# Where a diffusion trunk computes its adaLN modulation: as fills of the RWKV stage on TensorE, or on VectorE during the first projection

## The chip, the cores and the metric

The kernel runs on one core of one Trainium2 chip. The metric is device microseconds of one execution. A core has a matmul engine (TensorE, PE in the views), three elementwise engines (VectorE or DVE, ScalarE or ACT, GpSimd or POOL) and a queue engine (SyncE, SP) that here issues every transfer. Weights are loaded into the matmul engine by separate instructions (PEld in the views), which overlap with running matmuls.

## The reference, cut to what matters

One inference step over 128 context tokens and 1,024 latent tokens, width 1,024, two layers. Each layer norms its input, modulates it, projects it for four parallel mixers, mixes, projects back and adds the result through a gate. All three parts of the modulation are linear in a conditioning vector:

```python
sc_ctx = silu(c_ctx)             # context tokens
sc     = silu(c)                 # latent tokens
for l in range(2):
    mod = sc @ w_mod[l] + b_mod[l]          # (1024) @ (1024, 3072); once with sc_ctx, once with sc
    shift, scale, gate = split(mod, 3)      # 1024 each
    h = rmsnorm(x, norm_g[l]) * (1 + scale) + shift
    u = h @ w_in[l]                         # mLSTM, RG-LRU, retention, RWKV-7 inputs
    y = concat(mlstm(u), rglru(u), retention(u), rwkv(u)) @ w_out[l]
    x = x + gate * y
y = rmsnorm(x, final_g)
```

## The kernel before, in words

Activations lie with features on the 128 partitions and the 1,152 tokens along the rows. A layer has two long stages.

**First projection stage.** `in_proj` works through the list `JOBS` (one job for each block of 128 output features, or two blocks): 44 of its 56 jobs, since the RWKV inputs of head pairs 1 to 3 are left for later. A job loads its weights, splits them in two parts (ACT and POOL), and for each slice of 384 tokens accumulates 24 matmuls into a bank of PSUM with the tag `main`, of which there are two. DVE and ACT take turns to copy the bank to `st`, which is stored to memory. The mixers mLSTM, RG-LRU and retention (functions `ml_pair`, `lr_pair`, `rt_pair`, four head pairs each, one after the other) read these stores back and run on all engines at a higher priority, so the matmuls of `in_proj` fill what they leave free on TensorE.

**RWKV stage.** `rw_all` runs a long chain of small dependent steps. Here the order of the instructions on TensorE is written out by hand: a generator `work()` yields one matmul after the other of other work (the *fills*, line 1296), and `rw_all` pulls some of them at each step of its chain, so many that they last until its end (`nfill` is their number). The fills are the late RWKV projections (`late_proj`), the output projection (`out_proj`) and, in layer 0 alone, eight of the twelve blocks of the modulation. `tail` ends the layer.

**The modulation** has six blocks of 512 columns for each layer. Blocks 0 to 3 of layer 0 (shift and scale) are needed first and computed at the very start (`modulation0`). The other eight (`MODS`: the gate of layer 0, all of layer 1) are computed by `modulation`, in groups ahead of the late projections of pair 1, 2 and 3. `mod_rows` does a block: eight loads of 128 x 512 weights into the six buffers `ow`, eight fills with the two conditioning vectors (`silu_c`, 128 x 2) as TensorE's weights and the 512 columns streaming, which gives a row of 2 x 512; an ACT copy; four transposes; and a DVE addition of the bias into `mod`.

A float32 matmul is two instructions on TensorE here, so that a block's eight fills stand in the trace as 16 passes.

Outside the hand-made order a planner, which plays the program through on a timeline, orders each engine's instructions by priority: without a `high_priority` they come in the order of the code, with an offset of `HP1` or `HP2` ahead of that (`level(1)` is `HP1`, which is also what the mixers have; the copies of the projection have `HP2`).

Of the kernel before, what the change touches and what calls it, by code (L numbers as in the profile page):

```python
# [9 lines left out]
F32 = mybir.dt.float32  # L10
# [6 lines left out]
MUL, ADD, SUB, MAX, MIN = ALU.mult, ALU.add, ALU.subtract, ALU.max, ALU.min  # L17
# [13 lines left out]
class B:  # L31
# [1059 lines left out]
    def mod_rows(self, l, j, pool, w, n, pr, pc, mm, between=lambda k: None):  # L1091


        row_ps = pr()
        for k in range(0, 8, n):
            wt = w()
            self.dma(wt, self.i["w_mod"][l, j][:, k:k + n])
            between(k // n)
            for z in range(n):
                mm(row_ps[0:2], self.sc[:, k + z], wt[:, z], start=(k + z == 0), stop=(k + z == 7))  # L1100
                if k + z < 7:
                    yield
        row = pool.tile([2, 512], F32, tag="mrow", name="mrow", bufs=1)
        self.a.copy(row, row_ps[0:2])
        col_ps = pc()[:, 0:8].rearrange("p (i c) -> p i c", c=2)
        for i in range(4):
            self.tr(col_ps[:, i], row[:, 128 * i:128 * i + 128])
        self.tt(self.v, self.mod[l][:, 4 * j:4 * j + 4], col_ps,
                self.par["bmod"][:, 24 * l + 4 * j:24 * l + 4 * j + 4, None].broadcast_to([128, 4, 2]), ADD)
        yield  # L1110

    def modulation(self, l, j, pool):

        w = lambda: pool.tile([128, 1, 512], F32, tag="ow", name="wmod")
        yield from self.mod_rows(l, j, pool, w, 1, self.pmain, self.pmain, self.fill)

    def modulation0(self, pool, ps, between):

        bank = lambda n: lambda: ps.tile([128, 512], F32, tag=n, name=n)
        w = lambda: pool.tile([128, 2, 512], F32, tag="w0", name="w0", bufs=8)  # L1120
        for j in range(4):
            for _ in self.mod_rows(0, j, pool, w, 2, bank("row"), bank("col"), self.mm, lambda k: between(2 * j + k // 2) if k % 2 else None):
                pass

    def scales(self, l, pool):

# [120 lines left out]
        self.a.copy(hi, raw)  # L1247
        self.tt(self.g, lo, raw, hi.bitcast(F32), SUB)

    def in_proj(self, l, wp, sp, hh, hl):  # L1250
        n = 0
        rh = wp.tile([128, 3, KT, 128], F32R, name="wring_h")
        rl = wp.tile([128, 3, KT, 128], F32R, name="wring_l")
        pos = 0
        for t_, (kind, name, p, tiles) in enumerate(JOBS):
            if name[:3] == "rw_" and p in LATE:
                continue
            nt = len(tiles)
            if pos + nt > 3:
                pos = 0  # L1260
            with self.tc.high_priority(offset=HP2):
                for z, t in enumerate(tiles):
                    raw = wp.tile([128, KT, 128], F32, tag="raw", name="raw", bufs=2)
                    self.dma(raw, self.i["w_in"][l, t])
                    self.split_w(raw, rh[:, pos + z], rl[:, pos + z])
            hi, lo = rh[:, pos:pos + nt], rl[:, pos:pos + nt]
            pos += nt
            if kind == "C":
                dst = self.U[l, name, p] = self.dr0.tile([128, T], F32, name="u_%s_%d_%d" % (name, p, l))
                units = [(dst[:, o:o + CH3], slice(o, o + CH3), CH3) for o in range(0, T, CH3)]  # L1270
            else:
                dst = self.U[l, name, p] = self.dr0.tile([9, 128, 256], F32, name="ut_%s_%d_%d" % (name, p, l))
                units = [(dst[i], slice(128 * i, 128 * i + 128), 256) for i in range(9)]
            for d, s, w in units:
                ps = self.pmain()
                j = 0
                for k in range(KT):
                    for a, b in ((hi, hh), (hi, hl), (lo, hh)):
                        if kind == "C":
                            x, y = a[:, 0, k], b[:, k, s]  # L1280
                        else:
                            x, y = b[:, k, s], a[:, :, k]
                        self.mm(ps[:, :w], x, y, start=(j == 0), stop=(j == 3 * KT - 1))
                        j += 1
                with self.tc.high_priority(offset=HP2):
                    q = sp.tile([128, CH3], F32, tag="st", name="st", bufs=3)
                    if n % 2:
                        self.a.copy(q[:, :w], ps[:, :w])  # L1288
                    else:
                        self.v.tensor_copy(q[:, :w], ps[:, :w])  # L1290
                    n += 1
                    self.dma(d, q[:, :w])
# [66 lines left out]
    def build(self):  # L1359
# [10 lines left out]
        for l in range(2):  # L1370
# [6 lines left out]
            with self.ph as ph:  # L1377
                P = lambda n, b=1, **kw: ph.enter_context(tc.tile_pool(name=n + "_%d" % l, bufs=b, **kw, **tw))
                wp, sp = P("w"), P("st")
                self.in_proj(l, wp, sp, *self.h)  # L1380
                with tc.high_priority(offset=HP1), ExitStack() as st:
                    Q = lambda n, b=1, **kw: st.enter_context(tc.tile_pool(name=n + "_%d" % l, bufs=b, **kw, **tw))
                    self.mlrow = self.dr.tile([2, 40, T], F32, tag="mlrow", name="mlrow")
                    self.mldec = self.dr.tile([40, 9], F32, tag="mldec", name="mldec")
                    self.xps = Q("xps", 1, space=PSUM)
                    self.mp = Q("mp", **R)
                    self.ml_layer(l)
                    self.mq = Q("mq", **R)
                    for p in range(4):
                        self.ml_pair(l, p)  # L1390
                    with ExitStack() as st2:
                        Q = lambda n, b=1, **kw: st2.enter_context(tc.tile_pool(name=n + "_%d" % l, bufs=b, **kw))
                        self.lp = Q("lp", **R)
                        self.lr_layer(l, self.load_cols(self.lp, l, ("cw", "cb", "lam", "gb", "h0"), "lr_"))
                        self.lq = Q("lq", **R)
                        for p in range(4):
                            self.lr_pair(l, p)
                    with ExitStack() as st2:
                        Q = lambda n, b=1, **kw: st2.enter_context(tc.tile_pool(name=n + "_%d" % l, bufs=b, **kw))
                        self.tp = Q("tp", **R)  # L1400
                        self.rt_layer(l)
                        self.tq = Q("tq", **R)
                        for p in range(4):
                            self.rt_pair(l, p)
            fin = ExitStack()
            self.rf = fin.enter_context(tc.tile_pool(name="rw_fin_%d" % l, bufs=1, **R, **tw))
            with ExitStack() as ph:
                P = lambda n, b=1, **kw: ph.enter_context(tc.tile_pool(name=n + "_%d" % l, bufs=b, **kw, **tw))
                self.mainps = P("mo", 2, space=PSUM)
                wp, yp, sp = P("wo", OWB), P("yo", YOB), P("so", SO)  # L1410
                with tc.high_priority(offset=HP1):
                    self.rl, self.rp = P("rw_lora", **R), P("rw_pair", **R)
                    self.rt, self.rd = P("rw_tmp"), (P("rw_even"), P("rw_odd", **R))
                    self.rps = P("rw_ps", space=PSUM)
                    self.rw_layer(l, self.load_cols(self.rl, l, ("mu", "w0", "a0", "kk", "ka", "rk"), "rw_"))

                def work():
                    for p in LATE:
                        for z, j in MODS[p] if l == 0 else ():
                            yield from self.modulation(z, j, wp)  # L1420
                        yield from self.late_proj(l, p, wp, yp, sp)
                    yield from self.out_proj(l, ((0, 4), (1, 4), (2, 4)), wp, yp, sp)
                    while self.finished < 4:
                        yield
                    yield from self.out_proj(l, ((3, 3),), wp, yp, sp)
                    self.done.add("all")

                self.fills, self.done, self.credit, self.pulled, self.finished = work(), set(), 0.0, 0, 0
                self.nfill = 648 + (8 * sum(map(len, MODS.values())) if l == 0 else 0)
                self.rw_all(l)  # L1430
            self.tail(l, (3,), lambda: self.open_h(1))
            fin.close()
# [10 lines left out]

LATE, PROMPTS = (1, 2, 3), 6
OWB, SO = 6, 3
MODS = {1: ((0, 4), (0, 5)), 2: ((1, 0), (1, 1), (1, 2)), 3: ((1, 3), (1, 4), (1, 5))}
T12 = 2
LDB = dict(ld=2, ld2=2, y=1)
HP1 = 1000000
# [161 lines left out]
```

## Time and profile before

| | us |
|---|---|
| median of 3 runs | 3987.81 (3981.47 to 3994.23) |
| the profiled execution | 3979.25 |
| its span in the profile | 3977.5 |
| PE busy | 3648.6 (92%) |
| DVE busy | 2033.8 (51%) |
| ACT busy | 1291.7 (32%) |
| POOL busy | 1110.7 (28%) |

The profiled execution is 0.2% below the median of the runs. Times in the views count from the start of the span. "Busy" of TensorE is from the start of a matmul to its modelled end; matmuls overlap, so that many short ones in a row take less time than the sum of their durations.

### The profile page before, as it was taken

To read this page: it belongs to the slowest core of one execution; us is meant where nothing else is said; L and a number is where in the kernel's file an instruction comes from. 1 tells how busy PE (TensorE), PEld (TensorE's weight loads), DVE (VectorE), ACT (ScalarE), POOL (GpSimd) and SP (SyncE) were. 2 spreads that over 40 slices of the span, in tenths; PEclk is the share of its full clock that TensorE was granted. 3 is DMA by queue.
4 is the path that set the end of the run, shared out by engine and by line. 5 is a ranking of instruction groups with operands and counts; after the bars stand their busy time and mean duration, and the time that the engine had idled before them with its cause. 6 is when DMAs were issued, how large, how long until landed. Compare 5 with 4: busy or idle time off the path is not lost. (4 is left out here: it accounts for less than half of the span.)

```text
span 3977.5 us, 69524 instructions
## 1 busy us (share of the span) xinstructions
PE 3648.6 (92%) x28050; PEld 2831.0 (71%) x28050; DVE 2033.8 (51%) x3953; ACT 1291.7 (32%) x2102; POOL 1110.7 (28%) x1016
## 2 busy tenths in 40 slices
PE   6899999999899999998888999999997899989997
PEld 2899889999654555555468888999996555655554
DVE  4445544332364566675364545443423566766644
ACT  3234432212223334332142434422121334343313
POOL 4233234424331222212032232344243312122200
PEclk7999899989799999999989998999897999999998
DMA  5434343433356544344653443435333444434446
GB/s 214 122 106 137 121 132 120 141 111 120 127 156 187 146 141 134 109 124 123 198 189 118 104 120 124 129 121 146 106 122 119 133 151 133 141 101 126 129 128 201
DMA packets 413550, 538.02 MB, mean 135 GB/s; under 512 B 141708, under 2 KB 322700, under 8 KB 413228
## 3 DMA queue, kind: packets, MB, share of 16 engines
q1 hardware_dynamic: 413228, 533.57, 44.5%
q8 instruction: 221, 3.62, 0.4%
q14 instruction: 101, 0.83, 0.1%
HBM read 387.17 MB, written 146.25 MB: 134 GB/s over the span
## 5 line engine op out<-in xcount | busy, mean ns | idle before, releaser
L1296 PE MATMUL main<-yt,ow 128*128 128x384 f32 x2592 | 989.0, 520 | 25.1 <-DVE xi L48 17.5
L1296 PEld LDWEIGHTS main<-yt,ow 128*128 128x128 f32 x2592 | 478.0, 197 | 328.0 <-issue 49.1
L59 PE MATMUL main<-hh,wring_h 128*128 128x384 f32 x1824 | 648.1, 356 | 25.6 <-DVE st L1290 11.5
L59 PE MATMUL main<-hl,wring_h 128*128 128x384 f32 x1824 | 647.8, 355 | 21.7 <-DVE hl L44 19.6
L59 PE MATMUL main<-hh,wring_l 128*128 128x384 f32 x1824 | 644.1, 353 | 0.0
L44 POOL TENSOR_TENSOR wring_l<-raw,wring_h 128x1024 fp32r<-128x1024 f32 x100 | 246.8, 2472 | 605.1 <-ACT wring_h L1247 457.7
L59 PEld LDWEIGHTS main<-hh,wring_h 128*128 128x128 f32 x1824 | 360.8, 198 | 39.0 <-DVE st L1290 10.1
L59 PEld LDWEIGHTS main<-hl,wring_h 128*128 128x128 f32 x1824 | 361.1, 198 | 33.8 <-DVE hl L44 22.4
L59 PEld LDWEIGHTS main<-hh,wring_l 128*128 128x128 f32 x1824 | 360.7, 198 | 8.7 <-issue 2.7
L59 PE MATMUL main<-wring_h,hh 128*128 128x256 f32 x864 | 265.0, 307 | 17.7 <-DVE st L1290 17.1
L59 PE MATMUL main<-wring_h,hl 128*128 128x256 f32 x864 | 261.2, 302 | 0.0
L59 PE MATMUL main<-wring_l,hh 128*128 128x256 f32 x864 | 260.4, 301 | 0.0
L44 POOL TENSOR_TENSOR t<-s_k,bb 128x512 f32<-128x512 f32 x36 | 62.4, 1734 | 570.4 <-ACT bb L56 570.4
L1290 DVE COPY st<-main 128x384 f32<-128x384 f32 (+1 forms) x168 | 86.0, 512 | 261.8 <-PE main L59 222.5
L44 DVE TENSOR_TENSOR tm<-iU,iN 64x31 f32<-64x31 f32 (+15 forms) x558 | 202.2, 362 | 15.9
L44 DVE TENSOR_TENSOR iN<-iN,tm 64x31 f32<-64x31 f32 (+15 forms) x558 | 193.8, 347 | 15.8
L59 PEld LDWEIGHTS main<-wring_h,hh 128*128 128x128 f32 x864 | 178.0, 206 | 22.9 <-DVE st L1290 18.5
L59 PEld LDWEIGHTS main<-wring_h,hl 128*128 128x128 f32 x864 | 178.5, 207 | 4.5 <-issue 1.1
L59 PEld LDWEIGHTS main<-wring_l,hh 128*128 128x128 f32 x864 | 178.2, 206 | 2.7
L1247 ACT CAST wring_h<-raw 128x1024 fp32r<-128x1024 f32 x100 | 103.5, 1047 | 221.0 <-PE main L59 178.5
L1288 ACT COPY st<-main 128x384 f32<-128x384 f32 (+1 forms) x168 | 73.4, 437 | 270.2 <-PE main L59 264.3
L56 ACT ACT_TABLE_LOAD x123 | 157.8, 1283 | 2.9 <-PEq L1603 0.7
(332 smaller groups left out, 6040.2 us busy)
## 6 DMA issues: line engine op xcount, KB each, us to landing
raw<-in_w_in SPq DMA_DIRECT2D x100, 512.0 KB
ow<-in_w_in SPq DMA_DIRECT2D x144, 256.0 KB
ow<-in_w_out SPq DMA_DIRECT2D x144, 256.0 KB
yt<-h SPq DMA_DIRECT2D x144, 192.0 KB
mrb<-mlrow SPq DMA_DIRECT2D x48, 384.0 KB
x<-xi SPq DMA_DIRECT2D x96, 192.0 KB
yt<-y SPq DMA_DIRECT2D x90, 192.0 KB
wmod<-in_w_mod SPq DMA_DIRECT2D x64, 256.0 KB
```

What stands on the lines that cost most here:

```text
L44: return e.tensor_tensor(out=out, in0=a, in1=b, op=op)
L56: return self.a.activation(out=out, in_=a, func=f, scale=scale, bias=bias)
L59: return self.t.matmul(out, l, r, start=start, stop=stop)
L1247: self.a.copy(hi, raw)
L1288: self.a.copy(q[:, :w], ps[:, :w])
L1290: self.v.tensor_copy(q[:, :w], ps[:, :w])
L1296: return self.pe(self.t.matmul(*a, **k))
```

## The change

The eight blocks leave the generator of the RWKV stage, and `nfill` goes from 712 to 648 in layer 0. `in_proj` of layer 0 takes them in: at every fourth job it starts a block, and three jobs later it ends it. A block now loads its eight weight tiles into two buffers of its own, and DVE multiplies each by the conditioning value of its partition and adds it to a sum, one sum for each of the two conditioning vectors (a multiplication for the first tile, a `scalar_tensor_tensor` for each further one, 128 x 512 float32). After that TensorE sums over the partitions: eight matmuls with a 128 x 128 part of a sum as weights and one column of ones streaming. They go into a bank `main`, and DVE adds the bias. `modulation0` does what it did.

```diff
-                if k + z < 7:
-                    yield
...
+    def modulation(self, l, j, pool):
+        acc = [pool.tile([128, 512], F32, tag="macc%d" % e, name="macc") for e in range(2)]
+        with self.level(1):
+            for k in range(8):
+                w = pool.tile([128, 512], F32, tag="wmod", name="wmod", bufs=2)
+                self.dma(w, self.i["w_mod"][l, j][:, k])
+                for e in range(2):
+                    if k == 0:
+                        self.ts(self.v, acc[e], w, self.sc[:, k, e:e + 1], MUL)
+                    else:
+                        self.stt(self.v, acc[e], w, self.sc[:, k, e:e + 1], acc[e], MUL, ADD)
         yield
-    def modulation(self, l, j, pool):
-        w = lambda: pool.tile([128, 1, 512], F32, tag="ow", name="wmod")
-        yield from self.mod_rows(l, j, pool, w, 1, self.pmain, self.pmain, self.fill)
+        ps = self.pmain()[:, 0:8].rearrange("p (i c) -> p i c", c=2)
+        for i in range(4):
+            for e in range(2):
+                self.mm(ps[:, i, e:e + 1], acc[e][:, 128 * i:128 * i + 128], self.ones[:, 0:1])
+        self.tt(self.v, self.mod[l][:, 4 * j:4 * j + 4], ps,
+                self.par["bmod"][:, 24 * l + 4 * j:24 * l + 4 * j + 4, None].broadcast_to([128, 4, 2]), ADD)
...
-    def in_proj(self, l, wp, sp, hh, hl):
+    def in_proj(self, l, wp, sp, mp, hh, hl):
+        mods = [self.modulation(z, j, mp) for z, j in MODS] if l == 0 else []
...
+            if mods and t_ % 4 == 0:
+                next(mods[0])
+            if mods and t_ % 4 == 3:
+                next(mods.pop(0), None)
...
-                        for z, j in MODS[p] if l == 0 else ():
-                            yield from self.modulation(z, j, wp)
...
-                self.nfill = 648 + (8 * sum(map(len, MODS.values())) if l == 0 else 0)
+                self.nfill = 648
...
-MODS = {1: ((0, 4), (0, 5)), 2: ((1, 0), (1, 1), (1, 2)), 3: ((1, 3), (1, 4), (1, 5))}
+MODS = ((0, 4), (0, 5), (1, 0), (1, 1), (1, 2), (1, 3), (1, 4), (1, 5))
```

## Rows read from the trace of the kernel before

**Rows 1.** Busy time of each engine in stretches; layer 0's stages, layer 1's RWKV stage.

```profile
core 0: us, PE busy (x) PEld busy (x) DVE busy (x) ACT busy (x) POOL busy (x), PEclk, DMA share, GB/s
0.00:60.00 60.00, 37.18 (x87) 8.99 (x87) 18.30 (x38) 27.41 (x39) 13.22 (x16) 0.91 0.71 268
60.00:775.00 715.00, 674.01 (x3985) 629.28 (x3986) 347.64 (x528) 246.29 (x348) 255.05 (x232) 0.93 0.42 126
775.00:1040.00 265.00, 260.87 (x1573) 249.33 (x1572) 93.69 (x140) 58.72 (x93) 105.44 (x113) 0.93 0.37 118
1086.60:2032.00 945.40, 865.24 (x8364) 509.08 (x8364) 555.02 (x1284) 314.81 (x578) 182.54 (x139) 0.95 0.51 151
3074.50:3959.40 884.90, 804.80 (x8209) 497.58 (x8209) 544.36 (x1258) 306.01 (x556) 167.98 (x127) 0.95 0.46 137
```

**Rows 2.** Tile views: last mixer store, then last matmuls of tail, of each layer.

```profile
L81 SPq DMA_DIRECT2D y<-ng x1: 319/319/319, 1086.6 to 1086.6; - x1
...
L59 PE MATMUL main<-t_yl,t_hi x24: 333/337/629, 1992.2 to 2031.7; 128*128 128x384 f32 x24
...
L81 SPq DMA_DIRECT2D y<-ng x1: 320/320/320, 3074.5 to 3074.5; - x1
...
L59 PE MATMUL main<-t_yl,t_hi x24: 333/337/346, 3933.9 to 3959.0; 128*128 128x384 f32 x24
```

**Rows 3.** Tile view of the modulation's weights wmod, whole span.

```profile
L1296 PE MATMUL main<-wmod,silu_c x128: 591/592/1061, 1090.3 to 1415.7; 128*2 128x512 f32 x128
L81 SPq DMA_DIRECT2D wmod<-in_w_mod x64: 327/333/1074, 1040.8 to 1407.6; - x64
```

**Rows 4.** Groups by form, TensorE alone, RWKV stage of layer 0, then layer 1.

```profile
L1296 PE MATMUL main<-yt,ow 128*128 128x384 f32 x1296 | 490.7, 518 | 9.4 <-DVE xi L48 5.4 <-ACT xi L1329 2.4 <-PE main L1296 1.4
...
L1296 PE MATMUL main<-yt,ow 128*128 128x384 f32 x1296 | 498.2, 522 | 15.7 <-DVE xi L48 12.1 <-PE main L1296 1.9 <-ACT xi L1329 1.3
```

**Rows 5.** Timeline: fills of a modulation block and the transposes ahead of them.

```profile
1100.50 0.41 PE L62 MATMUL main<-ident,mrow 2*128 2x2 f32 x4
...
1100.84 5.31 PE L1296 MATMUL main<-wmod,silu_c 128*2 128x512 f32 x12
```

**Rows 6.** Timeline: float32 passes with 128x128 weights, between projections, then alone.

```profile
1038.76 1.48 PEld L59 LDWEIGHTS rup<-rtV,rkw 128*128 128x128 f32 x12
...
1040.16 0.19 PEld L59 LDWEIGHTS main<-hl,wring_h 128*128 128x128 f32 x1
...
1053.24 0.55 PEld L59 LDWEIGHTS rN<-rtV,rsd 128*128 128x128 f32 x2
...
1053.66 0.55 PEld L59 LDWEIGHTS rN<-rtR,rtQX 128*128 128x128 f32 x2
```

**Rows 7.** Timeline: DVE operations of 128 x 512, and a POOL operation beside one.

```profile
1088.96 0.43 DVE L52 TENSOR_SCALAR tw<-tw 128x512 f32<-128x512 f32 x1 [2.43 <-ACT tw L56]
...
1104.73 0.68 DVE L48 SCALAR_TENSOR_TENSOR t<-kk,bb 128x512 f32<-128x512 f32 x1
...
1108.46 1.85 POOL L44 TENSOR_TENSOR BK<-ta,t 128x256 f32<-128x256 f32 x2
...
1109.65 1.21 DVE L48 SCALAR_TENSOR_TENSOR t<-kk,bb 128x512 f32<-128x512 f32 x1
```

**Rows 8.** Waits of TensorE in the first projection stage: us, times, longest.

```profile
PE main L59 <- DVE st L1290: 14.9, 5, 5.8
```

**Rows 9.** Timeline of SP's queue: where one mixer's pair ends and the next begins.

```profile
669.69 0.32 SPq L81 DMA_DIRECT2D y<-ng  x1
...
723.05 1.75 SPq L81 DMA_DIRECT2D QQ<-u_ml_q  x3
...
866.61 0.43 SPq L81 DMA_DIRECT2D y<-ng  x1
...
873.20 9.96 SPq L81 DMA_DIRECT2D u_rt_q<-st  x2
884.75 0.32 SPq L81 DMA_DIRECT2D rtq<-u_rt_q  x1
```

More of the change, by code (lines that the diff above doesn't have):

```diff
@@ L1121, in modulation0 @@
         for j in range(4):
-            for _ in self.mod_rows(0, j, pool, w, 2, bank("row"), bank("col"), self.mm, lambda k: between(2 * j + k // 2) if k % 2 else None):
-                pass
+            self.mod_rows(0, j, pool, w, 2, bank("row"), bank("col"), self.mm, lambda k: between(2 * j + k // 2) if k % 2 else None)
     def scales(self, l, pool):
@@ L1379, in build @@
                 wp, sp = P("w"), P("st")
-                self.in_proj(l, wp, sp, *self.h)
+                self.in_proj(l, wp, sp, P("md") if l == 0 else None, *self.h)
                 with tc.high_priority(offset=HP1), ExitStack() as st:
```

## The prediction

> **What bounds the kernel now.** I read the busy times by stretch first, with one stretch for each stage [rows 1]. From 60 to 1,040 us, the first projection stage of layer 0, TensorE is busy for 674.01 of 715 us and then for 260.87 of 265 us. TensorE sets the end of that stage; DVE has work for half of it (347.64 of 715 us). Next I looked for the two ends of the RWKV stage that both layers have in common: the store of the last mixer, and the last matmul of `tail` [rows 2]. Between them lie 945.4 us in layer 0 and 884.9 us in layer 1. That pair of stretches is the centre of the argument, since layer 1 runs the same code there without the modulation. The third view is the tile view of the modulation's weights [rows 3]: all 128 passes lie between 1,090 and 1,416 us, so nothing of the blocks to be moved lies outside this stage. The other fills are the same in both layers, 1,296 passes of nearly the same length [rows 4].
>
> The reader should see in the two stretches [rows 1] that TensorE idles for 945.4 - 865.24 = 80.2 us in layer 0 and for 884.9 - 804.8 = 80.1 us in layer 1. The granted share of the clock is 0.95 in both. So the fills of the modulation don't sit in gaps of the chain that would otherwise stay empty: without them the stage is shorter by as much as TensorE is less busy.
>
> **What leaves the RWKV stage.** Twelve passes of 128 x 2 weights and 512 streamed columns take 5.31 us, 0.44 us each [rows 5]; 128 of them take 56.6 us. Four transposes take 0.41 us [rows 5], so eight blocks 3.3 us. Together that is 59.9 us of TensorE's hand-made order, and the difference of the two layers is 945.4 - 884.9 = 60.5 us. Two readings that share no number agree, so I take -60.5 us. The ACT copies of the row, the bias additions on DVE and the 64 loads [rows 3] go too; they lie beside this work and I give nothing for them. The bounds: were the fills free, the gain would be 0, which the equal idle time speaks against; if layer 1 was luckier by chance, some 10 us less. The upper end I set at 70 us, for loads that compete with others: the stage moves 151 GB/s against 137 GB/s without them [rows 1].
>
> **What comes into the first projection stage.** Layer 0 pays for three things there.
>
> *TensorE.* Each block adds eight float32 matmuls, 16 passes, with a 128 x 128 weight and a single column. No such form is in the trace. The nearest is a pass with the same weights and 64 columns: in the midst of the projection's matmuls twelve take from 1038.76 to 1040.16 us, 0.117 us each [rows 6]. 128 passes are 15 us; with the granted share of 0.93 in this stage, 16 us. From below: nothing, if they fall in the 41 us in which TensorE has no work before 775 us [rows 1]. From above: later, outside the projection's stream, two such passes take 0.42 us [rows 6], 0.21 us each, 27 us for all. I take 16 us, because the new passes stand in that stream.
>
> *DVE.* Each block adds 14 operations of two tensors and two of one. The nearest rows have the same size: 0.68 us for a `scalar_tensor_tensor` and 0.43 us for a one-tensor operation [rows 7]. A block costs 14 x 0.68 + 2 x 0.43 = 10.4 us, all eight 83 us. DVE idles for 715 - 347.64 = 367 us in the stretch that takes them [rows 1], and the copies of the projection's banks keep a higher priority. So I cost the 83 us at nothing on the path; what hides them is TensorE's projection work, which is there to be done whenever a mixer is late. What they cost without that cover is the first rival.
>
> *The bank and the queue.* A block takes a turn of the two `main` banks. Its 16 passes last 1.9 us, so the bank of the projection before it has to be copied out in that time, where it had a whole turn of 24 matmuls until now; and the bias addition that frees the block's bank has no raised priority, so it queues on DVE behind whatever a mixer has ready. TensorE has waited for DVE's copies in this stage 5 times, 14.9 us in all [rows 8], so some 3 us where it happens. I take 1 us for each of eight blocks, 8 us; bounds 0 and 24 us (every block waits 3 us). The 64 loads issue at 0.33 us each [rows 3] and their 64 x 0.26 MB arrive in a stretch that moves 126 GB/s; a load of the new kind waits for a buffer on SP, and the stores of `st` and the weight loads of the projection are behind it there. With two buffers only the first 0.5 MB can come up during the start, where the memory delivers 268 GB/s [rows 1]: 2 us if they delay the first norm, 0 if they don't. I take 1 us.
>
> **The sum.** -60.5 + 16 + 8 + 1 = -35.5 us. From the profiled execution's 3979.25 us this makes 3943.8 us. The median of the runs is 8.6 us above that execution, so the forecast of the median is 3987.8 - 35.5, rounded to 3952 us. With the ends of the terms the saving lies between 50 - 27 - 24 - 2 = -3 and 70 us; since they hardly all meet, the likeliest case has its own range of 3936 to 3973 us.
>
> **Rival 1, slower: the mixers become late in the first stage.** The four retention pairs run one after the other. Pair 2 starts at 884.75 us, when its data has just been stored (873 to 883 us), and pair 1 was done at 866.61 us; mLSTM's pair 3 starts at 723.05 us, pair 2 was done at 669.69 us [rows 9]. So the mixers have 18 us of slack at the later place and 53 us at the earlier one. If DVE's 83 us all land on this chain, 83 - 18 = 65 us are left over, and the sum is -60.5 + 16 + 9 + 65 = +29.5 us, 4017 us. It decides the sign once 35.5 us of the excess are on the chain, that is 54 of the 83 us. What makes it dearer is seen in the rows: the same operation took 1.21 us with POOL at work beside it, 0.68 us alone [rows 7]. At 1.21 us the blocks cost DVE 8 x (14 x 1.21 + 2 x 0.43) = 142 us, 142 - 18 = 124 us over the slack, and the end is at 4076 us. POOL is busy for 255 of the 715 us [rows 1], so about a third of the operations meet it. Against this rival: six of the eight blocks are started before the first retention job, and what the mixers lose there they regain in the 53 us ahead of mLSTM's pair 3; only 21 us (two blocks) fall behind that. Chance 0.10.
>
> The Trainium skill, "SBUF — State Buffer", section "SBUF: two separate sides", says that a VectorE operation with two inputs in SBUF and a GpSimd operation that reads SBUF take one pair of ports from each other for the length of an instruction, the loser standing still. The two durations just named agree with that, and by this rule POOL's weight splits would be held up as well; with it this rival would weigh more, and I keep its chance at 0.10, since the splits are made one or two jobs ahead.
>
> **Rival 2: the RWKV stage gives back less.** Layer 0's chain might be limited elsewhere once the fills are gone; the change would then not do what it is meant to. At half the gain the sum is -30 + 25 = -5 us, 3983 us; at none, +25 us, 4013 us. For it: the chain of small steps is long, and TensorE waits in it for 80 us. Against it: layer 1 is that case, and it idles no longer. Chance 0.10, three fifths of it near half the gain.
>
> **Rival 3: the sums cost nothing.** The 16 passes of a block fall into waits that TensorE has anyway, and the bank is free in time: -60.5 + 1 = -59.5 us, 3928 us. For it: 41 us without work before 775 us [rows 1]. Against it: much of that lies in the first 40 us, while the norm is still being computed, and from 775 us on TensorE is busy for 98%. Chance 0.10.
>
> **How the numbers follow.** My forecast has 0.70. A measurement of this kernel tells about 0.3%, 12 us, from no change; so faster means below 3976 us. The forecast's case is there but for 0.04 (its bounds met together); rival 3 is all faster; rival 2 gives 0.06 to no change and 0.04 to slower, rival 1 all to slower. Faster 0.76, same 0.10, slower 0.14. The range goes from 3922 us (rival 3 and 6 us) to 3984 us; it leaves out rival 1, the worse half of rival 2, and some 0.04 at the ends.
>
> **What would show it.** Right: the RWKV stage of layer 0, measured between the same two events, lasts about 885 us, with no pass on the modulation's weights after 1,090 us; 112 `scalar_tensor_tensor` of about 0.7 us stand on DVE before 800 us; 128 short passes with one column on TensorE, about 0.12 us apart; the last mixer store comes some 25 us later than 1086.6 us. Wrong: that store comes over 60 us later with retention pairs that start behind each other instead of behind their data (rival 1); the stage stays above 915 us with TensorE idling for more than 110 us (rival 2); the store doesn't move (rival 3). TensorE waiting for bias additions on DVE, or the first norm ending later, would show that the third term is too small. What I can least see is how the planner rearranges the first stage: it lays out every engine anew, and a different order there could be worth as much as the terms above.

## The result, and the profile after

The changed kernel is slower: 4003.84 us as the median of 20 runs (3988.92 to 4016.49), beside 3980.14 us (3962.87 to 3998.76) for 20 runs of the kernel before. The ratio is 1.0059 with an interval of 1.0044 to 1.0075, about +23.5 us. Its profiled execution took 4012.55 us, span 4010.8 us, 33.3 us over that of before. It is one of the longer of the 20, so sizes below are taken from ratios where there are any, and the profile tells where the time lies.

I cut the span at events that both kernels have: the first operation of layer 0's norm on DVE, the last store of mLSTM's gate input (`u_ml_g`), the last store of RWKV's gate input (`u_rw_g`, the end of `in_proj`), the last mixer store, and the end of `tail`. First the changed kernel's busy times in these stretches (columns as in [rows 1]), layer 1's two stages last:

```profile
62.10:877.90 815.80, 734.12 (x4245) 683.37 (x4246) 449.90 (x675) 257.30 (x371) 286.90 (x266) 0.90 0.46 131
1125.30:1170.90 45.60, 29.01 (x121) 25.77 (x122) 8.58 (x13) 7.22 (x10) 11.95 (x22) 0.52 0.39 123
1170.90:2065.20 894.30, 808.83 (x8204) 500.13 (x8204) 549.57 (x1274) 308.73 (x565) 178.72 (x136) 0.94 0.47 140
2065.20:3093.50 1028.30, 967.20 (x5701) 901.73 (x5700) 447.89 (x679) 325.62 (x474) 374.03 (x371) 0.92 0.42 125
3093.50:3992.60 899.10, 813.19 (x8208) 502.18 (x8208) 546.46 (x1259) 306.06 (x556) 167.48 (x127) 0.94 0.45 134
```

And the kernel before, the two stretches that [rows 1] cut elsewhere:

```profile
53.30:792.10 738.80, 691.79 (x4104) 645.60 (x4105) 358.24 (x553) 257.08 (x371) 268.78 (x259) 0.93 0.42 125
1041.70:1086.60 44.90, 27.73 (x121) 24.55 (x122) 8.59 (x13) 7.22 (x10) 11.96 (x22) 0.54 0.38 125
```

Four differences make up the 33.3 us of the two profiled executions:

- **First projection stage, +84.3 us.** The last mixer store of layer 0 comes at 1170.9 us, not 1086.6 [rows 2]. The norm begins 8.8 us later (62.1 for 53.3), and the stretch to the last `u_ml_g` store is 77.0 us longer. Behind that nothing is lost: 1125.3 - 877.9 = 247.4 us to the last `u_rw_g` store for 249.6 us before, then 45.6 for 44.9 us.
- **RWKV stage of layer 0, -51.1 us** (894.30 for 945.4 [rows 1]).
- **Layer 1's first stage, -14.2 us, and its RWKV stage, +14.2 us** (899.10 for 884.9 [rows 1]), though the diff leaves both alone. They cancel.

In the stretch that lost 77 us TensorE idles for 815.80 - 734.12 = 81.7 us, 34.7 us more than before (738.80 - 691.79 = 47.0). Its busy time grew by 42.3 us, of which the new column sums are 8 x 1.92 = 15.4 us by the timeline below; the other 27 us are the old matmuls at a lower granted clock, 0.90 for 0.93. So less than half of TensorE's loss stands where TensorE waits.

The waits of TensorE there in the changed kernel (us in total, times, longest), to be held against [rows 8]:

```profile
PE main L59 <- DVE st L1307: 25.5, 9, 10.5
...
PE mS L59 <- DVE mrb L44: 9.8, 4, 3.5
...
PE mup L59 <- DMA mV<-ut_ml_vo: 7.1, 1, 7.1
```

The rows of this view sum to 87.0 us, before to 47.7 us. TensorE waits for DVE's copies of its banks (the first row) 9 times instead of 5, for 10.6 us more than before. The larger part is at the mixers' own matmuls, all rows whose output isn't `main`: 33.2 us in 15 waits, before 9.8 us in 6. Not all of those wait for DVE; 7.1 us are for a mixer's load.

The longest wait for a copy, 10.5 us, has no sum ahead of it. TensorE's row at its end, then what DVE did until then:

```profile
145.20 0.58 PE L59 MATMUL main<-wring_h,hh 128*128 128x256 f32 x1 [10.53 <-DVE st L1307]
```

```profile
135.11 4.25 DVE L738 TENSOR_TENSOR_SCAN mg_m<-mg_lf,mg_m,mg_ig 8x1024 f32<-8x1024 f32 x1
139.39 2.55 DVE L734 TENSOR_TENSOR_SCAN mg_F<-mg_mk,mg_lf 8x1152 f32<-8x1152 f32 x1
141.95 2.55 DVE L735 TENSOR_TENSOR_SCAN mg_F<-mg_mk,mg_lf 8x1152 f32<-8x1152 f32 x1
...
144.61 0.54 DVE L1307 COPY st<-main 128x384 f32<-128x384 f32 x1
```

These are scans of mLSTM's gates. The kernel before has the same scans at this place, with a wait of 5.8 us [rows 8].

What the sums themselves do to DVE shows the tile view of `macc`, which also lists what DVE stood idle for ahead of them:

```profile
L59 PE MATMUL main<-ones,macc x128: 166/250/353, 132.8 to 852.7; 128*128 128x1 f32 x128
L48 DVE SCALAR_TENSOR_TENSOR macc<-wmod,silu_c,macc x112: 733/745/2840, 33.2 to 772.4; 128x512 f32<-128x512 f32 x112
L52 DVE TENSOR_SCALAR macc<-wmod,silu_c x16: 474/486/2943, 32.3 to 754.1; 128x512 f32<-128x512 f32 x16
...
  DMA wmod<-in_w_mod: 38.6, 25
```

DVE stood 25 times, 38.6 us in all, in front of a sum whose weights were not there yet: 24.9 us in 19 of these waits lie in the stretch that lost 77 us, the other 6 ahead of the norm. What is queued behind such a sum waits too. At the start this can be followed in DVE's timeline (start, us, last in brackets the idle time before it and its releaser):

```profile
46.50 4.83 DVE L48 SCALAR_TENSOR_TENSOR macc<-wmod,silu_c,macc 128x512 f32<-128x512 f32 x4 [7.41 <-DMA wmod<-in_w_mod]
...
60.12 1.41 DVE L48 SCALAR_TENSOR_TENSOR macc<-wmod,silu_c,macc 128x512 f32<-128x512 f32 x2 [1.22 <-DMA wmod<-in_w_mod]
61.45 0.16 DVE L44 TENSOR_TENSOR mod<-col,p_bmod 128x8 f32<-128x8 f32 x1
...
62.13 7.06 DVE L48 SCALAR_TENSOR_TENSOR xs<-xs,sg,rstd 128x128 f32<-128x128 f32 x17
```

The last transposes of `modulation0` were started on TensorE at 55.96 us and took 0.41 us, but the bias addition that the norm needs stands on DVE behind sums that wait for their loads, until 61.45 us. Before, these transposes were started at 52.13 us, so 3.8 of the norm's 8.8 us were lost ahead of them and the other 5 us on DVE.

The price of the column sums themselves came out as forecast. TensorE's timeline of one block (the bracketless form: start, us, engine, operation):

```profile
132.66 1.92 PEld L59 LDWEIGHTS main<-ones,macc 128*128 128x128 f32 x16
132.83 1.84 PE L59 MATMUL main<-ones,macc 128*128 128x1 f32 x16
```

That is 0.12 us a pass, the figure read from [rows 6].

### The profile page after: what moved, and what is told of

Same layout as the page of the kernel before. It is cut to its first block, busy times and chain, and to the rows that moved or that the text cites. A ratio compares the mean times of both kernels' runs of the same rounds, so it can differ in the third digit from the quotient of the medians.

```text
span 4010.8 us, 69601 instructions
## 1 busy us (share of the span) xinstructions
PE 3637.2 (91%) x28018; PEld 2855.0 (71%) x28018; DVE 2129.2 (53%) x4081; ACT 1288.6 (32%) x2094; POOL 1120.9 (28%) x1016
## 5 line engine op out<-in xcount | busy, mean ns | idle before, releaser
L1313 PE MATMUL main<-yt,ow 128*128 128x384 f32 x2592 | 1004.2, 525 | 24.1 <-DVE xi L48 16.7
L59 PEld LDWEIGHTS main<-hl,wring_h 128*128 128x128 f32 x1824 | 363.4, 199 | 24.0 <-DVE hl L44 12.1
L59 PE MATMUL main<-wring_h,hh 128*128 128x256 f32 x864 | 264.1, 306 | 26.4 <-DVE st L1307 24.9
L44 DVE TENSOR_TENSOR tm<-iU,iN 64x31 f32<-64x31 f32 (+15 forms) x558 | 205.6, 368 | 15.4
L44 DVE TENSOR_TENSOR iN<-iN,tm 64x31 f32<-64x31 f32 (+15 forms) x558 | 193.6, 347 | 15.6
L1307 DVE COPY st<-main 128x384 f32<-128x384 f32 (+1 forms) x168 | 85.9, 511 | 208.2 <-PE main L59 167.1
L56 ACT ACT_TABLE_LOAD x123 | 157.8, 1283 | 2.9 <-PEq L1618 0.7
```

The lines of the kernel that those rows point to most:

```text
L44: return e.tensor_tensor(out=out, in0=a, in1=b, op=op)
L56: return self.a.activation(out=out, in_=a, func=f, scale=scale, bias=bias)
L59: return self.t.matmul(out, l, r, start=start, stop=stop)
L1313: return self.pe(self.t.matmul(*a, **k))
```

## The experiments

Twelve kernels ran. The ratio is to the kernel before; the third column is the time of the last mixer store of layer 0 in the one profiled execution of each (before 1086.6, after 1170.9).

| kernel | ratio (95%) | store, us |
|---|---|---|
| after | 1.0059 (1.0044 to 1.0075) | 1170.9 |
| x1_noload | 0.9993 (0.9972 to 1.0015) | 1122.7 |
| x2_nodve | 0.9934 (0.9909 to 0.9958) | 1111.8 |
| x3_nope | 0.9961 (0.9938 to 0.9984) | 1129.9 |
| x4_low | 1.0026 (1.0006 to 1.0046) | 1151.1 |
| y1_bias | 1.0037 (1.0017 to 1.0057) | 1157.1 |
| y2_bufs | 0.9973 (0.9951 to 0.9995) | 1134.0 |
| y3_start | 1.0030 (1.0007 to 1.0053) | 1148.9 |
| y4_none | 0.9910 (0.9874 to 0.9946) | 1085.8 |
| z1_all | 0.9992 (0.9964 to 1.0020) | 1123.7 |
| t8_tail | 0.9947 (0.9920 to 0.9975) | 1097.4 |
| t4_tail | 0.9943 (0.9917 to 0.9970) | 1097.2 |

`before_again` is the kernel before, profiled a second time, with no ratio.

### One part of the block left out

**x1_noload**: one load in place of 64; the sums use that tile.

```diff
-                w = pool.tile([128, 512], F32, tag="wmod", name="wmod", bufs=2)
-                self.dma(w, self.i["w_mod"][l, j][:, k])
+                if not hasattr(self, "w1"):
+                    self.w1 = pool.tile([128, 512], F32, tag="wmod", name="wmod", bufs=1)
+                    self.dma(self.w1, self.i["w_mod"][l, j][:, k])
+                w = self.w1
```

> The changed kernel with one load of modulation weights in the first projection stage instead of 64; all DVE sums and column sums stay and work on that one tile (the modulation's values are so left out). Theory A (DVE's time: 128 operations of 0.74 us stand in DVE's queue ahead of the mixers and the bank copies, TensorE waits, and its granted clock falls) expects only the part that hangs on loads to go: the start (8.8 us) and DVE's waits for loads, so the last mixer store of layer 0 at 1145 to 1160 us (1170.9 in the changed kernel, 1086.6 before), ratio to before 0.998 to 1.003. Theory B (the 64 loads: SP's queue and DVE standing at loads) expects that store at 1100 to 1115 us, ratio 0.985 to 0.99.

**x2_nodve**: DVE's 128 operations are left out; the two sums are filled once with a constant, while loads and column sums stay.

```diff
+        if not hasattr(self, "acc1"):
+            self.acc1 = [pool.tile([128, 512], F32, tag="macc%d" % e, name="macc") for e in range(2)]
+            for a in self.acc1:
+                self.v.memset(a, 0.01)
+        acc = self.acc1
...
-                for e in range(2):
-                    if k == 0:
-                        self.ts(self.v, acc[e], w, self.sc[:, k, e:e + 1], MUL)
-                    else:
-                        self.stt(self.v, acc[e], w, self.sc[:, k, e:e + 1], acc[e], MUL, ADD)
```

> The changed kernel without the 128 DVE operations of the sums: the sums are filled once with a constant, the 64 loads go into their two buffers with no reader, and the column sums stay (the modulation's values are so left out). Theory A expects the last mixer store of layer 0 at 1100 to 1115 us and a ratio of 0.985 to 0.992. Theory B expects it at 1135 to 1165 us, ratio 0.995 to 1.003. Theory C (the column sums and their turn of the bank) expects it above 1140 us.

**x3_nope**: the column sums are left out; the bias is added to eight columns of a sum.

```diff
-        ps = self.pmain()[:, 0:8].rearrange("p (i c) -> p i c", c=2)
-        for i in range(4):
-            for e in range(2):
-                self.mm(ps[:, i, e:e + 1], acc[e][:, 128 * i:128 * i + 128], self.ones[:, 0:1])
+        ps = acc[0][:, 0:8].rearrange("p (i c) -> p i c", c=2)
```

> The changed kernel without the 64 matmuls of the column sums and their bank; the bias is added to eight columns of a sum instead (the sum over partitions is left out). Theory A and B expect the 16 us of the matmuls to go and no more: the last mixer store of layer 0 at 1150 to 1158 us, ratio 1.001 to 1.004. Theory C expects it at 1100 to 1125 us, ratio below 0.996.

The stretch from the norm to the last `u_ml_g` store, in x1_noload, x2_nodve and x3_nope:

```profile
58.10:828.50 770.40, 717.53 (x4245) 669.49 (x4246) 433.26 (x675) 258.00 (x371) 284.84 (x265) 0.91 0.40 120
```

```profile
58.30:824.70 766.40, 706.49 (x4244) 659.84 (x4245) 345.85 (x563) 257.07 (x371) 275.36 (x266) 0.93 0.46 139
```

```profile
64.60:841.20 776.60, 708.99 (x4123) 657.42 (x4124) 441.82 (x670) 257.59 (x371) 292.23 (x271) 0.91 0.46 137
```

Each of the three gives back a large part: 0.66% (26 us), 1.25% (50 us) and 0.98% (39 us) of the time. These sum to 115 us, and y4_none below puts the whole cost of the blocks at 0.0149, 59 us. So the parts do not add, and none of the theories A, B and C fits all three kernels. They are no clean removals either, since the planner moved what was left: the 64 loads of x2_nodve are all issued by 157.8 us, and the sums of x3_nope all run before 297 us, in the changed kernel until 773 us. In x2_nodve TensorE has the clock of before, 0.93, and the gaps are 766.40 - 706.49 = 59.9 us; in x1_noload they are 52.9 us, still with the full DVE work and a clock of 0.91.

The waits for bank copies in the stretch (as in [rows 8]) are in x2_nodve as long as in the changed kernel, although no sum stands on DVE there:

```profile
PE main L59 <- DVE st L1306: 27.8, 6, 13.3
```

### Priority, bias, buffers, start

**x4_low**: loads and sums at the projection's own priority.

```diff
-        with self.level(1):
+        with self.level(0):
```

> The changed kernel with the loads and the DVE sums at the priority of the projection's own code instead of the mixers' (level 0 for level 1), so that the planner puts them behind the mixers' operations wherever both are ready. Theory A expects much of the stage back, the last mixer store of layer 0 at 1110 to 1140 us and a ratio of 0.988 to 0.998, provided that the order is what costs. If DVE's time is what costs in whatever order, or theory B or C holds, it stays at 1155 us or later, ratio 1.001 or more.

A third of a per cent comes back (1.0059 to 1.0026). The mixers' priority alone is not what costs: DVE still waits 24 times, 32.2 us in all, for loads of the sums.

**y1_bias**: the bias addition, which frees the block's bank, at the priority of the bank copies.

```diff
-        self.tt(self.v, self.mod[l][:, 4 * j:4 * j + 4], ps,
-                self.par["bmod"][...].broadcast_to([128, 4, 2]), ADD)
+        with self.tc.high_priority(offset=HP2):
+            self.tt(self.v, self.mod[l][:, 4 * j:4 * j + 4], ps,
+                    self.par["bmod"][...].broadcast_to([128, 4, 2]), ADD)
```

> The changed kernel with the bias addition that frees a block's bank at the priority of the bank copies (HP2); nothing is left out. In the changed kernel TensorE stands after the column sums until a bank is free: 10.8, 3.4, some 8 and 3.4 us at four of the eight blocks, and the bias addition comes 0.7 to 11.7 us after the last sum. Theory C' (the turn of the bank, held by a late bias addition) expects 15 to 30 us back: the last mixer store of layer 0 at 1141 to 1156 us (1170.9), ratio 0.998 to 1.003. Theory A' (the copies themselves stand behind the sums and scans in DVE's queue) expects under 8 us, ratio 1.004 or more.

1.0037 against 1.0059: the intervals overlap, so at most a small gain. TensorE's waits for DVE's bank copies are not fewer, as its line of TensorE's waits shows:

```profile
PE main L59 <- DVE st L1308: 29.0, 9, 10.6
```

So nothing here shows the bank that the block turns to be the main cost.

**y2_bufs**: six load buffers for two, nothing else.

```diff
-                w = pool.tile([128, 512], F32, tag="wmod", name="wmod", bufs=2)
+                w = pool.tile([128, 512], F32, tag="wmod", name="wmod", bufs=6)
```

> The changed kernel with six buffers for the modulation's weights instead of two, so that a load is issued well ahead of its use; nothing is left out. If the loads cost because DVE stands at them with mixers and copies queued behind (38.6 us, 25 times in the changed kernel), most of what the kernel with one load gave back returns here: the last mixer store at 1125 to 1145 us, ratio 0.998 to 1.002. If they cost through SP's queue and the memory, or through the start, it stays above 1155 us, ratio 1.003 or more; the start gets later still, since six loads instead of two go ahead of those of the first norm.

This single number turns the sign: 0.9973, faster than before, 0.86% (34 us) below the changed kernel. The tile view of its sums has DVE's waits for loads at

```profile
  DMA wmod<-in_w_mod: 8.3, 2
```

where two buffers had 38.6 us in 25 waits. Both lie ahead of the norm, so that none is left in the stretch. The stretch from the norm to the last `u_ml_g` store and the wait of TensorE for bank copies:

```profile
62.40:839.90 777.50, 720.58 (x4245) 672.09 (x4246) 433.93 (x675) 258.43 (x371) 283.11 (x265) 0.91 0.47 136
```

```profile
PE main L59 <- DVE st L1307: 20.2, 4, 10.6
```

It is 38.3 us shorter with the same instructions: TensorE idles 56.9 us instead of 81.7, and its busy time falls from 734.12 to 720.58 us with the clock at 0.91 instead of 0.90. The start is not mended (62.4 us): here the last bias addition of `modulation0` waits for its transposes on TensorE, 7.18 us.

**y3_start**: the first block begins at job 4 instead of 0, the last ends at job 35.

```diff
-            if mods and t_ % 4 == 0:
+            if mods and t_ >= 4 and t_ % 4 == 0:
...
-            if mods and t_ % 4 == 3:
+            if mods and t_ >= 4 and t_ % 4 == 3:
```

> The changed kernel with the first block started at job 4 instead of job 0, and all others one turn later; nothing is left out. The first norm began at 62.1 us in the changed kernel and at 53.3 us before, with the first block's loads and DVE sums ahead of it. If the loads and sums at the start cause that and the planner doesn't pull them forward again, the first norm begins at 53 to 55 us and the ratio is 1.002 to 1.005; if the planner issues them as early as buffers allow, since nothing else holds them back, the start stays at 60 us or later.

The norm still begins at 62.9 us: the planner issued the first loads as early as before, since nothing holds them. Yet the store comes 22 us earlier and the ratio is 1.0030. One block's column sums fall behind the last `u_ml_g` store here, which explains only some 2 us; the rest is another order of the same work, and this run can't say which part of it.

**z1_all**: six buffers, the bias at the bank copies' priority, and the first six loads held until the norm is done (ACT writes one column of the tile from the norm's last output, so that the load must come after it).

```diff
-                w = pool.tile([128, 512], F32, tag="wmod", name="wmod", bufs=2)
+                w = pool.tile([128, 512], F32, tag="wmod", name="wmod", bufs=6)
...
+                if (l, j) == MODS[0] and k < 6:
+                    self.a.copy(w[:, 0:1], self.h[1][:, KT - 1, T - 1:T].bitcast(F32))
```

> The changed kernel with the three remedies together: six buffers for the modulation's weights, the bias addition at the priority of the bank copies, and the first six loads held back by a small copy of the norm's last output into their tiles, so that the first norm isn't late; nothing is left out. If the three costs add up (-34, -9 and -6 to -9 us in ratios measured for each or read from the start), the ratio is 0.991 to 0.996, the first norm begins before 57 us and the last mixer store of layer 0 comes at 1115 to 1130 us. If DVE's time is what is left, the ratio stays at 0.996 to 0.999.

The start is mended (52.7 us) and DVE waits for loads only 4.5 us, but the ratio is 0.9992, not to be told from y2_bufs' 0.9973. The three remedies don't add. The stretch to the last `u_ml_g` store is as long as y2_bufs', 780.3 us, and TensorE still waits for bank copies:

```profile
PE main L59 <- DVE st L1310: 24.0, 7, 12.5
```

### The removal alone, and a second profile of before

**y4_none**: the eight blocks are left out of both stages; `mod` gets the bias only.

```diff
-        acc = [pool.tile([128, 512], F32, tag="macc%d" % e, name="macc") for e in range(2)]
-        with self.level(1):
...
-        self.tt(self.v, self.mod[l][:, 4 * j:4 * j + 4], ps, ...)
+        self.ts(self.v, self.mod[l][:, 4 * j:4 * j + 4], self.par["bmod"][...].broadcast_to([128, 4, 2]), 0.0, ADD)
```

> The changed kernel with the eight blocks of the modulation left out altogether (the bias alone is written): neither fills in the RWKV stage nor loads, sums and column sums in the projection stage. It isolates the first term of the prediction, -60.5 us, that is a ratio of 0.985 (0.983 to 0.987), with the last mixer store of layer 0 at 1080 to 1095 us and 885 to 895 us from there to the end of tail's matmuls. If the moved fills were worth less, the ratio is 0.988 or more.

> The kernel before, profiled once more. The prediction took the RWKV stage of layer 1 (884.9 us) as what layer 0's would last without the modulation; in all profiles since then, of kernels with the same code in layer 1, that stage lasts 889 to 899 us. If 884.9 us was a low draw of the same plan, this profile shows 888 to 899 us for layer 1 and 940 to 955 us for layer 0, and the prediction's first term was too large by chance. If the planner's order in the kernel before is the better one, it shows 883 to 887 us again.

First layer 0's first stretch and the RWKV stages of both layers without the blocks, then the same RWKV stages in the second profile of before:

```profile
55.80:791.20 735.40, 689.24 (x4103) 642.99 (x4104) 352.06 (x553) 257.52 (x371) 271.30 (x259) 0.94 0.42 126
1085.80:1978.60 892.80, 804.85 (x8205) 498.35 (x8204) 549.49 (x1275) 309.40 (x566) 179.06 (x137) 0.95 0.47 141
3016.60:3911.00 894.40, 808.47 (x8209) 499.12 (x8209) 545.14 (x1258) 306.51 (x556) 168.14 (x127) 0.95 0.45 135
```

```profile
1073.70:2017.80 944.10, 862.41 (x8364) 508.29 (x8364) 554.35 (x1284) 313.48 (x574) 181.18 (x136) 0.95 0.50 151
3059.50:3940.50 881.00, 804.71 (x8209) 497.90 (x8209) 544.49 (x1258) 306.70 (x556) 167.58 (x127) 0.95 0.46 137
```

With the work simply gone, the ratio is 0.9910 (0.9874 to 0.9946), 36 us, not 60. TensorE's busy time in layer 0's stage falls to 804.85 us, 60.4 us less than [rows 1] and to within 0.2 us of the 804.71 us of layer 1. But the stage takes 892.80 us, so TensorE idles for 88 us in it, where [rows 1] have 80. And layer 1's stage, of which the diff touches nothing, takes 894.40 us for 884.9 and 881.00 us in the two profiles of before. So of the 24 us that the ratio lacks, 8 us are missing in the stage itself and some 10 us are lost in layer 1.

### Other places for the blocks

**t8_tail**: the kernel before, with all eight blocks in their old form (conditioning vectors as weights, 512 columns streaming) issued behind the last projection job, into TensorE's gaps at the end of the first stage; six buffers, the first loads held as in z1_all. **t4_tail**: four blocks there and four in the RWKV stage, two ahead of pair 2 and two ahead of pair 3.

```diff
+    def modulation_tail(self, l, j, pool, n):
...
+        for _ in self.mod_rows(l, j, pool, w, 1, self.pmain, self.pmain, self.mm):
+            pass
...
+        if l == 0:
+            cnt = []
+            for z, j in TAILMODS:
+                self.modulation_tail(z, j, mp, cnt)
...
-MODS = {1: ((0, 4), (0, 5)), 2: ((1, 0), (1, 1), (1, 2)), 3: ((1, 3), (1, 4), (1, 5))}
+TAILMODS = ((0, 4), (0, 5), (1, 0), (1, 1), (1, 2), (1, 3), (1, 4), (1, 5))
+MODS = {1: (), 2: (), 3: ()}
```

That is t8_tail; t4_tail differs in the two lists alone:

```diff
+TAILMODS = ((0, 4), (0, 5), (1, 0), (1, 1))
+MODS = {1: (), 2: ((1, 2), (1, 3)), 3: ((1, 4), (1, 5))}
```

> The kernel before with all eight blocks in their old form (fills with the conditioning vectors as weights, row copy, transposes), but issued behind the last job of the first projection stage of layer 0, at the projection's priority, with six buffers for the loads; nothing is left out. After its last matmul that stage goes on for 45 us with TensorE busy for 28 of them at a granted clock of 0.54, waiting for the last retention pair. If the blocks' 60 us fill this, the last mixer store comes at 1085 to 1115 us, the RWKV stage takes 887 to 895 us, and the ratio is 0.990 to 0.996. If the RWKV stage waits for the blocks to end, they cost there what they cost before: ratio 0.997 to 1.003.

> As the kernel with eight blocks behind the projection, but with four there and four still among the fills of the RWKV stage (two ahead of pair 2, two ahead of pair 3). The four take 30 us of TensorE, which the 45 us of the retention pair's end can hide: ratio 0.991 to 0.995. If what is hidden there is given back in the RWKV stage, 0.997 to 1.002.

From the last `u_rw_g` store to the last mixer store, t8_tail, then t4_tail:

```profile
1039.00:1097.40 58.40, 54.74 (x218) 21.67 (x217) 9.22 (x17) 10.02 (x15) 12.05 (x22) 0.97 0.79 266
```

```profile
1044.80:1097.20 52.40, 46.99 (x202) 20.87 (x201) 9.21 (x17) 9.53 (x14) 12.04 (x22) 0.97 0.71 238
```

Both beat both kernels: 0.9947 and 0.9943, some 21 and 23 us under the kernel before. In the same stretch the kernel before left TensorE idle for 44.90 - 27.73 = 17.2 us at a granted clock of 0.54; with blocks in it TensorE idles for 3.7 and 5.4 us at 0.97, and the stretch is only 13.5 and 7.5 us longer. Four of the eight blocks do as much as all eight: in t8_tail only 80 of the 128 passes, five blocks, fit ahead of the last mixer store. The other 48 run until 1125 us in the RWKV stage, which takes 901.0 us, more than the 887 to 895 us expected.

## Why the prediction was wrong

**The step that failed** is the one on DVE in the change part by part: "So I cost the 83 us at nothing on the path; what hides them is TensorE's projection work, which is there to be done whenever a mixer is late". The work was sized a little low (112 sums took 85.9 us and 16 multiplications 15.6 us, 101.5 us for 83). Its cover was not there: the kernel without this work (x2_nodve) is 50 us faster than the changed one. Nor does TensorE turn to the projection whenever a mixer is late: it has its order from the planner too, and it stood 33.2 us at mixers' matmuls, before 9.8 us. I had set DVE's work against DVE's idle time and left out that DVE can idle *with* work in its queue, as it did 25 times in front of its sums. The waits of the kernels side by side, in the stretch from the norm to the last `u_ml_g` store, all in us and each the sum of the rows of its view (x3_nope is left out, since its sums end before 297 us):

| kernel | stretch | DVE waits for loads of sums | TensorE waits at mixers' matmuls | TensorE waits for DVE's bank copies |
|---|---|---|---|---|
| before | 738.8 | none | 9.8 | 14.9 |
| y4_none | 735.4 | none | 9.1 | 14.5 |
| after | 815.8 | 24.9 | 33.2 | 25.5 |
| x4_low | 804.4 | 26.1 | 28.1 | 21.8 |
| y1_bias | 802.8 | 21.7 | 27.1 | 29.0 |
| y3_start | 792.3 | 20.9 | 14.8 | 27.7 |
| z1_all | 780.3 | 4.4 | 12.2 | 24.0 |
| y2_bufs | 777.5 | 0 | 12.1 | 20.2 |
| x1_noload | 770.4 | 0 | 7.5 | 18.2 |
| x2_nodve | 766.4 | no sums | 4.6 | 27.8 |

Among the kernels that compute or load for the blocks, the stretch goes with the waits at mixers' matmuls, and these, but for y3_start, with DVE's waits for loads; the waits for bank copies don't follow it. The four kernels with over 20 us of load waits have ratios from 1.0026 to 1.0059, the three others with sums 0.9973 to 0.9993: some 20 us between the means of the two groups, each kernel with an order of its own. That the path leads from the late sum over a late mixer to TensorE's wait is read from these rows and not followed wait by wait.

The same mistake is in the queue's term: I asked what two buffers do to SP and to the start (1 us), and not what they do to DVE, which is at most two tiles from its next wait. In the same stretch SP stands 49.4 us in 33 waits until a sum frees a load buffer, and with six buffers still 41.4 us in 30, so SP's queue is not what six buffers relieved.

The ratios give the sizes, each step the difference of two kernels times some 3975 us:

| step | forecast | measured |
|---|---|---|
| blocks taken out (y4_none to before) | -60.5 | -36 (±14) |
| blocks put in, six buffers (y2_bufs to y4_none) | +25 | +25 (±17) |
| two buffers for six (after to y2_bufs) | 0 | +34 (±11) |
| together | -35.5 | +23.5 |

Here ± is the root of the squared half widths of the two intervals; the first and last line have that of their own ratio. The middle line has just the sum that I had given to column sums, bank turn and start together. I call that luck: the bound is wide, and the late start and DVE's work itself are in it. Of the 34 us below it, some 20 are what the two groups above show to go with the waits for loads; the rest can be the order that the planner gave the changed kernel, the slowest of its group.

**The costs do not add.** With D for DVE's sums, L for loads and C for column sums and their bank, the ratios above y4_none are C + L 0.0024 (x2_nodve), D + L 0.0051 (x3_nope), D + C 0.0083 (x1_noload). Were they to add, all three would cost half their sum, 0.0079, 31 us; measured is 0.0149, 59 us. The other 28 us (±12) come in only where parts meet; how much of them is instead the order into which the planner put what was left in x2_nodve and x3_nope is open. In the profile TensorE's gaps bring 35 us, and in the same stretch the granted clock falls from 0.93 to 0.90, which goes with 27 us more of busy time. That the gaps lower the clock is argued, not shown: gaps of 47.0, 56.9 and 81.7 us go with 0.93, 0.91 and 0.90, but 52.9 us in x1_noload go with 0.91 and 59.9 us in x2_nodve with 0.93.

**Column sums, 16 us:** 1.92 us a block, 15.4 us as work, right. **Bank turn, 8 us:** TensorE's waits for DVE's copies grew by 10.6 us, and y1_bias finds no clear gain in freeing the bank sooner; the term was not what failed. **Start and queue, 1 us:** too small; 8.8 us in the profile, mended in z1_all, though without a gain in the ratio that can be told from none.

**RWKV stage, -60.5 us:** right in kind, too large. In y4_none TensorE's busy time fell by what was read from the trace, 60.4 us, and 8 us came back as idle time; the stage lasted 892.8 us, not 885. That "layer 1 is that case" held for TensorE's work, but not for the time of layer 1 itself: in all changed kernels layer 1's own stage is longer too, 889 to 899 us, while before_again gives 881.0 us, so the 884.9 us was no lucky draw. TensorE's order in layer 1's stage is the same before and after but for 2 of some 8,200 matmuls, and DVE's isn't: 47 of its 1,247 operations stand elsewhere, in before_again 1. That the planner's other order costs those 10 us fits, but no run isolates it. In the changed kernel it is 14.2 us, which layer 1's first stage won back.

**Rival 1** (slower, 4017 us) had the sign, the engine and nearly the time, but not the path. It asked for mixers that run past their slack at the end of the stage, with retention pairs starting behind each other. Pair 2 still starts behind its data (stores from 953.94 to 964.25 us, its first load at 965.84, pair 1 done at 952.40), and the end of `in_proj` itself is late, with the same 45 us behind it. **Rival 2** (the stage gives back less) holds for 8 to 10 us: the stage lasts 894.3 us (892.8 in y4_none) and not above 915; the rest of what the ratio of y4_none lacks lies elsewhere. **Rival 3** (the sums cost nothing) is out: the store moved by 84 us. My note that the planner's new order "could be worth as much as the terms above" was the honest part of it: y3_start moved the store by 22 us, with 18 us less of waits at mixers' matmuls, for no cause that I can name.

**Left open:** why z1_all's remedies don't add to y2_bufs; what y3_start gained; and whether layer 1's extra time is DVE's order. Which steps of the mixers each wait of TensorE goes back to was not followed. Sums that are issued only once their load has landed were not tried.

## What to carry to other kernels

An engine's idle share is no cover for new work that waits on transfers: what counts is how far ahead the loads run, since what is queued behind waits too. Nor is work of the critical engine a cover if its order is laid out beforehand: here TensorE stood at the mixers' matmuls. Before giving work to an engine, count the buffers of its loads: here six for two were worth 34 us (±11), beside 25 us (±17) for everything else that was added. And work that must be done some time can go where the critical engine stands idle anyway: here the end of a stage took four blocks in their old form for 7.5 us.

## What the runs showed of the hardware

**Sums beside GpSimd.** The sums took 0.745 us in the middle but up to 2.84 us. One such place in the changed kernel, DVE's timeline, then POOL's:

```profile
465.17 1.41 DVE L48 SCALAR_TENSOR_TENSOR macc<-wmod,silu_c,macc 128x512 f32<-128x512 f32 x2
...
469.45 4.16 DVE L48 SCALAR_TENSOR_TENSOR macc<-wmod,silu_c,macc 128x512 f32<-128x512 f32 x3
```

```profile
469.38 2.37 POOL L44 TENSOR_TENSOR wring_l<-raw,wring_h 128x1024 fp32r<-128x1024 f32 x1 [11.90 <-ACT wring_h L1259]
```

Two sums alone take 1.41 us; three beside a weight split on POOL take 4.16 us, 2.05 us more than three at that rate, for a split of 2.37 us. The Trainium skill, "SBUF — State Buffer", section "SBUF: two separate sides", has a VectorE operation with two SBUF inputs and a GpSimd one that reads SBUF shut each other out for a whole instruction; these rows agree. With a mean of 0.81 us for the 112 sums it is the exception here: the dear price of rival 1, 1.21 us for each sum, did not come true.

**A gap filled costs little.** The stretch at the end of the first stage ran at a granted clock of 0.52 to 0.54 with TensorE at 62 to 64% busy, and at 0.97 with four or five blocks in it at 90 to 94%: in t8_tail 27 us more of busy time made the stretch 13.5 us longer.
